# Sums of gates in six shared weight buffers, turns that meet, a norm by token tile and a re-ordered table in a transformer block

## The chip, the cores and the metric

The kernel runs on one core of one Trainium2 chip. The metric is the time of the device in microseconds (us) for one execution. Five engines run their own streams: TensorE (PE, matmuls), VectorE (DVE), ScalarE (ACT), GpSimd (POOL) and SyncE (SP, which issues most transfers). They meet at semaphores, and each works through its stream in the order in which it was written.

## What is computed

One block on x (256 tokens by 2048 channels), float32 throughout, with a conditioning vector c. Cut to what matters:

```python
mod = silu(c) @ w_ada + b_ada                  # w_ada 2048 x 12288
sh1, sc1, g1, sh2, sc2, g2 = split(mod, 6)     # parts 0..5 of the kernel
h = rms_norm(x, norm1_g) * (1 + sc1) + sh1
q, k, v, gb, gc, xt = split(h @ w_in, 6)       # each 256 x 1024; the kernel's q k v g c x
attn = softmax(mask(rms(q) @ rms(k).T / sqrt(128))) @ v     # 8 heads
conv = gb * causal_dwconv(gc * xt, conv_w, conv_b)          # 3 taps
mixed = concat(rms_norm(attn), rms_norm(conv))
x = x + g1 * (mixed @ w_out)                   # 2048 x 2048
h2 = rms_norm(x, norm2_g) * (1 + sc2) + sh2
u = causal_dwconv(h2 @ w_ffn_up, ffn_conv_w, ffn_conv_b)    # 2048 x 11264
x = x + g2 * ((silu(u_gate) * u_up) @ w_ffn_down)           # 5632 x 2048
```

## The kernel before

Nearly all of the work is one pass over 315 MB of weights. They arrive in raw tiles of 128x2048 float32 (1 MB, `raw`, a ring of 5 buffers, issued from SP's queue). A matmul on float32 is done as three faster ones: ACT rounds a tile to `hi` (L246), DVE takes the rest `lo` = raw - hi (L252), the activations are split in the same way (`h` and `hl`, `mixh` and `mixl`), and PE adds h x hi, hl x hi and h x lo. A ring of 3 holds hi and lo, and they are made two slots ahead of their use.

A **slot** is one weight tile, about 5.5 us of PE. There are 48 slots for `w_in` (0 to 47), 16 for `w_out` (48 to 63), 88 for `w_ffn_up` in pairs (64 to 151: a group of channels has two halves of k), and 48 for `w_ffn_down`. In slot i the loop at the end of the file first writes hi of slot i+2 and the small tasks that are due (before or after lo, by a class), then PE's matmuls of slot i, then the tiles of `w_ada` ("ada"). The table `CFG` holds the due slots, classes and orders, so the order on each engine follows from it.

What the change and the steps touch:

- **turns** (`CFG['turns']`): in which order the six products of `w_in` take their slots. Where the next turn of a product isn't in the next slot, its PSUM bank is emptied into an SBUF sum `pa_*` (ACT copy L424 the first time, DVE addition L426 after that).
- **ada**: the six vectors of the modulation. Some chunks are accumulated on PE (L297), the rest on DVE (L301 and L303, scalar times row plus sum, 16 rows of 128 of w_ada to a sum). The sums of the gates (parts 2 and 5) are 2048 wide and stand in a tile of their own; their bias comes by eight 1x512 transfers and eight additions (L325).
- **attention, conv**: mix tiles with their squares (L996, L1015); the last square's sum goes at once to PE (`ssA`, `ssC`, L1022), for the norms of the two halves. The conv's three taps are one ACT operation and two DVE ones (L1075 to L1078).
- **the end of w_out** (slots 62 and 63, bank `m('C', 3)`): DVE adds the product to x (L501, L506), ACT squares it (L508), the root, `n2d` and one matmul `n2b` (L606) spread 1/rms over the partitions, ACT copies it to `rB` (L610), and `h_chunks` write h2 (DVE L629, ACT L631, DVE L634), which the first `z` (L795) waits for. Four ada tiles (`fill`) are PE's work in between.
- **up**: each group's two slots hold their h x hi as 16 matmuls 512 wide (h and hl in one, L795) and h x lo as 16 that are 256 wide (L798); ACT and DVE add the two halves of a bank (`ub`, L685 and L688). With `direct` a slot's products go to one 256-wide half instead, and there is no addition on DVE.
- **spill**: the eight tiles of x are written to the output by ACT's queue (L541) between up slots, and read back for the end.

Of the kernel before, what the change touches and what calls it, by code (L numbers as in the profile page):

```python
# [1270 lines left out]
```

## Time and profile before

| | us |
|---|---|
| median of 3 runs (1179.96 to 1181.82) | 1180.21 |
| the profiled execution, its own time | 1182.36 |
| its span in the trace | 1180.5 |
| PE busy | 1153.6 |
| DVE busy | 934.8 |
| ACT busy | 620.3 |

The span is what the trace covers; the profiled execution took 1.86 us more than its span. Busy PE is not PE at its peak, since matmuls overlap; the spacing of equal matmuls in a row says what one costs. [...]

### The profile page before, as it was taken

The numbers are of one execution on the slowest core, as the hardware profiler recorded it, in microseconds if no ns is written. First come the engines' busy times: TensorE is split into PE (matmuls) and PEld (weight loads), VectorE is DVE, ScalarE is ACT, GpSimd is POOL, SyncE is SP. The second block draws the span as 40 slices with busy tenths as digits, with TensorE's granted clock in tenths as the row PEclk, the third lists the DMA queues.
The fourth block names the chain that finished last, engine by engine and source line by source line (L and its number), as shares of the span: only waits on it lengthen the run. The fifth ranks groups of instructions, "written<-read, shape, count | busy, mean of one in ns | idle before, by whom it ended". The sixth has DMA issues, their size and how long they took to land.

```text
span 1180.5 us, 15371 instructions
## 1 busy us (share of the span) xinstructions
PE 1153.6 (98%) x5971; PEld 964.6 (82%) x5971; DVE 934.8 (79%) x1060; ACT 620.3 (53%) x890; POOL 1.2 (0%) x8
## 2 busy tenths in 40 slices
PE   5999999999999999999999999999999999999998
PEld 3777788878877878888888888888888888888887
DVE  3588999999999989989988766887655676576876
ACT  5645265468584555476665434555444455335442
...
GB/s 364 382 348 389 384 344 376 414 366 319 319 280 308 285 297 330 384 237 155 178 222 259 372 324 319 234 195 179 194 230 172 189 179 208 234 210 203 135 169 89
DMA packets 189181, 317.98 MB, mean 269 GB/s; under 512 B 6922, under 2 KB 106028, under 8 KB 184756
## 3 DMA queue, kind: packets, MB, share of 16 engines
...
## 4 chain that ended last, share of the span: by engine, by line
PE 81%; DVE 10%; DMA 4%; ACT 2%; issue 1%; SPq 0%; ACTq 0%; DVEq 0%
PE z L795 23%; PE z L798 12%; DVE lo L252 4%; DVE ada L303 3%; DMA raw<-in_w_in_dram 2%; PE ada L297 1%; PE mg L414 1%; PE mg L415 1%; PE mg L412 1%; PE mx L414 1%; DMA raw<-in_w_ffn_up_dram 1%; PE mx L415 1%; PE mx L412 1%; DMA raw<-in_w_ada_dram 1%; PE mc L414 1%
## 5 line engine op out<-in xcount | busy, mean ns | idle before, releaser
L252 DVE TENSOR_TENSOR lo<-raw,hi 128x2048 fp32r<-128x2048 f32 (+2 forms) x204 | 448.2, 2204 | 141.5 <-ACT hi L246 125.4
L246 ACT ACTIVATE hi<-raw 128x2048 fp32r<-128x2048 f32 (+2 forms) x204 | 376.1, 1850 | 299.5 <-DMA raw<-in_w_in_dram 80.0
L795 PE MATMUL z<-h,hi 128*128 128x512 f32 x1408 | 329.7, 390 | 2.6 <-DVE h L634 2.0
L795 PEld LDWEIGHTS z<-h,hi 128*128 128x128 f32 x1408 | 261.1, 188 | 56.2 <-DVE h L634 1.4
L303 DVE SCALAR_TENSOR_TENSOR ada<-raw,csil,ada 128x512 f32<-128x512 f32 (+2 forms) x150 | 183.8, 1229 | 3.3 <-DMA raw<-in_w_ada_dram 0.2
L798 PEld LDWEIGHTS z<-h,lo 128*128 128x128 f32 x1408 | 174.8, 192 | 3.4
L798 PE MATMUL z<-h,lo 128*128 128x256 f32 x1408 | 176.0, 283 | 0.0
L688 DVE TENSOR_TENSOR ub<-z,ub 128x256 f32<-128x256 f32 x112 | 39.6, 417 | 34.4 <-ACT ub L685 34.3
L685 ACT ACTIVATE ub<-z 128x256 f32<-128x256 f32 x112 | 33.4, 383 | 35.3 <-PE z L795 35.3
L720 ACT ACTIVATE gh<-uy 128x512 fp32r<-128x512 f32 x22 | 13.9, 632 | 66.8 <-DVE uy L718 66.8
L702 ACT ACTIVATE uy<-ub,fc,fc 128x256 f32<-128x256 f32 x88 | 45.6, 600 | 1.9 <-DVE ub L693 1.9
L709 DVE SCALAR_TENSOR_TENSOR uy<-ub,fc,uy 128x254 f32<-128x254 f32 x88 | 42.5, 484 | 3.1
L707 DVE SCALAR_TENSOR_TENSOR uy<-ub,fc,uy 128x255 f32<-128x255 f32 x88 | 42.1, 479 | 0.1
L297 PE MATMUL ada<-raw,crep 128*32 128x256 f32 (+1 forms) x224 | 23.1, 530 | 7.6 <-DMA raw<-in_w_ada_dram 7.6
L714 ACT ACTIVATE uy<-uy 128x512 f32<-128x512 f32 x22 | 13.8, 627 | 29.7 <-DVE uy L709 29.7
L721 DVE TENSOR_TENSOR gl<-uy,gh 128x512 fp32r<-128x512 f32 x22 | 15.2, 693 | 15.4 <-ACT gh L720 15.4
L414 PE MATMUL mc<-hi,h 128*128 128x512 f32 x64 | 25.6, 400 | 1.1 <-ACT pa_x L424 1.1
L414 PE MATMUL mv<-hi,h 128*128 128x512 f32 x64 | 25.4, 397 | 0.7 <-ACT h L864 0.7
L414 PE MATMUL mg<-hi,h 128*128 128x512 f32 x64 | 25.7, 401 | 0.0
L414 PE MATMUL mx<-hi,h 128*128 128x512 f32 x64 | 25.4, 397 | 0.0
L414 PE MATMUL mk<-hi,h 128*128 128x512 f32 x64 | 25.3, 396 | 0.0
L415 PE MATMUL mq<-hi,hl 128*128 128x512 f32 x64 | 25.0, 391 | 0.2 <-DVE hl L869 0.2
...
## 6 DMA issues: line engine op xcount, KB each, us to landing
...
```

Of the source, the lines that this page charges most:

```text
L246: act(hi[:, :nk], t[:, :nk], AF.Copy)
L252: V.tensor_tensor(out=lo[:, :nk], in0=t[:, :nk], in1=hi[:, :nk].bitcast(F32), op=ALU.subtract)
L297: mm(self.acc[q:q + 32, :], crep[:, i, :], t[:, j, :], start=(r == 0 and j < 4), stop=(r == self.tiles - 1 and j >= self.rows - 4), tile_p ...
L303: V.scalar_tensor_tensor(out=self.acc, in0=t[:, j, :], scalar=csil[:, i:i + 1], in1=self.acc, op0=ALU.mult, op1=ALU.add)
L414: mm(o, a, hi[:, k, s], start=(first and k == 0), stop=False)
L415: mm(o, b, hi[:, k, s], start=False, stop=False)
L688: V.tensor_tensor(out=d, in0=zp[grp][ft][:, :256], in1=d, op=ALU.add)
L702: act(y, b, AF.Identity, bias=fcols[3][:, i:i + 1], scale=fcols[2][:, i:i + 1])
L707: V.scalar_tensor_tensor(out=y[:, 1:], in0=b[:, :255], scalar=fcols[1][:, i:i + 1], in1=y[:, 1:], op0=ALU.mult, op1=ALU.add)
L709: V.scalar_tensor_tensor(out=y[:, 2:], in0=b[:, :254], scalar=fcols[0][:, i:i + 1], in1=y[:, 2:], op0=ALU.mult, op1=ALU.add)
L795: mm(zp[grp][ft], hi[:, j, ft * P:(ft + 1) * P], h2T[k + j], start=begins and j == 0, stop=ends and j == 3)
L798: mm(zp[grp][ft][:, :256], lo[:, j, ft * P:(ft + 1) * P], h2T[k + j][:, :256], start=False, stop=False)
```

## The change

- The table has other numbers: turns, heads, due slots, classes, which raw tiles are loaded first (`x_first`) and where hi is written late (`hi_late`). The first loads, up to the eleventh raw tile, differ in one place only: slot 4's weights go ahead of an ada tile.
- `near` 1 to 3: a product's bank is kept if its next turn is up to three slots away. `direct` [0,0] to [1,0]: in groups 0 to 5 the slots of the first half of k write into 256-wide halves, so their 12 slots have 48 matmuls of 256 instead of 16 of 512 and 16 of 256.
- Buffers: raw 5 to 6, but the 2048-wide sums of the gates live in a raw tile (`home`, zeroed on POOL, with the bias row brought by POOL's queue), so five are left while a gate is summed. The eight bias transfers and additions go.
- One 256-wide chunk of part 1 is summed on DVE (16 operations 256 wide) instead of PE (two tiles of 16 matmuls).
- The sums of squares go to PE one slot later (`sslag`); squares and mix tiles of attention go in pairs, 512 wide.
- The last bank of w_out, and the last ones of w_ffn_down, are split in two halves of 256 with banks of their own; the norm after w_out goes by token tile, and `rB` is copied behind the first two chunks of h2.
- One tap of the short conv goes to ACT, the small vectors come by POOL's queue six slots earlier, and some small copies from PSUM move from DVE to ACT. The spills stand at slots 72, 74, 76, 78 instead of 69 to 72.

```diff
-         [4, 8, 512, False, 54, 7], [1, 2, 256, True, 0, 3], ...
+         ... [1, 8, 1024, False, 8, 12], [1, 2, 256, False, 1, 2], ...
- 'bufs': [42, 6, 5, 3, 3],
+ 'bufs': [38, 6, 6, 3, 5],
+ 'taps': [1, 0, 0],
+ 'sslag': 1,
- 'near': 1,
+ 'near': 3,
- 'direct': [0, 0],
- 'spill': [5, 1],
+ 'direct': [1, 0],
+ 'spill': [8, 2],
...
     def load_next():
         if pending:
+            if isinstance(pending[0], Ada):
+                pending.pop(0).home()
+                return
...
+        def home(self):
+            what = f"ada{self.part}_{self.c0}"
+            self.acc = sb.tile([P, 4, 512], F32, tag="raw", bufs=N_RAW, name=what).rearrange("p a b -> p (a b)")
+            nc.gpsimd.memset(self.acc, 0.0)
+            a = self.part * D + self.c0 * P
+            nc.gpsimd.dma_start(self.acc[0:1, :], b_ada[0:1, a:a + self.n])
...
+        one(0, slice(0, 512), 0)
+        one(1, slice(0, 256), 1)
+        root(0, 0)
+        one(1, slice(256, 512), 2)
+        nrm["p"] = bank("n2b")
+        diag(0)
+        root(1, 2)
+        diag(1)
...
-        p = bank("n2b")
-        mm(p[:, :256], ones, d, start=True, stop=True)
+        for t in range(2):
+            mm(p[:, t * P:(t + 1) * P], ones, nrm["d", t], start=True, stop=True)
...
+        ks = list(range(cut[0]))
+        h2_chunks(ks[:2], p[:, :256])
         act(rB[0], p[:, :256], AF.Copy)
-        h2_chunks(range(cut[0]), p[:, :256])
+        h2_chunks(ks[2:], rB[0])
...
+            if CFG["sslag"]:
+                at(now[0] + CFG["sslag"], ss_cols, w)
```

ACT at slots 1 to 3, before (`hi` is the rounding of a weight tile, `pa_x` and `pa_c` empty the banks of slots 2 and 3, `adae` a bank of an ada sum):

```order
L313 ACTIVATE adae_2_400<-ada_2_312 128x256
L246 ACTIVATE hi<-raw 128x2048
L424 ACTIVATE pa_x_456<-mx_402 128x512
L424 ACTIVATE pa_x_458<-mx_403 128x512
L424 ACTIVATE pa_x_460<-mx_416 128x512
L424 ACTIVATE pa_x_462<-mx_417 128x512
L313 ACTIVATE adae_2_468<-ada_2_323 128x256
L424 ACTIVATE pa_c_510<-mc_470 128x512
L424 ACTIVATE pa_c_512<-mc_471 128x512
```

and now (the banks of slots 1 and 2 are `mc` and `mv`):

```order
L255 ACTIVATE hi<-raw 128x2048 x2
L431 ACTIVATE pa_c_380<-mc_333 128x512
L431 ACTIVATE pa_c_382<-mc_334 128x512
L431 ACTIVATE pa_c_384<-mc_347 128x512
L431 ACTIVATE pa_c_386<-mc_348 128x512
L431 ACTIVATE pa_v_440<-mv_392 128x512
L431 ACTIVATE pa_v_442<-mv_393 128x512
L431 ACTIVATE pa_v_444<-mv_406 128x512
L431 ACTIVATE pa_v_446<-mv_407 128x512
L329 ACTIVATE adae_2_448<-ada_2_314 128x256
L255 ACTIVATE hi<-raw 128x2048
```

The banks of slot 2 were emptied behind hi of slot 5; they are now emptied ahead of it, behind hi of slot 4.

PE at the end of slot 49, before (`m('A', 1)` and `m('A', 0)` are banks of w_out, `adab` spreads a gate, `trg` transposes for the conv):

```order
L412 MATMUL m('A', 1)1_2937<-lo,mix_2150 128x512
L369 MATMUL adab_0_2964<-ada_0_1535,ones 128x512
L1022 MATMUL ssA<-ones,sq 128x1 x2
L1064 MATMUL trg_2982<-ident,pa_g_392 128x128
L1064 MATMUL trg_2982<-ident,pa_g_394 128x128
```

and now, at the end of slot 51:

```order
L422 MATMUL m('A', 1)1_2867<-hi,mixl 128x512
L419 MATMUL m('A', 1)0_2866<-lo,mixh 128x512
L419 MATMUL m('A', 1)1_2867<-lo,mixh 128x512
L419 MATMUL m('A', 1)0_2866<-lo,mixh 128x512
L419 MATMUL m('A', 1)1_2867<-lo,mixh 128x512
L419 MATMUL m('A', 1)0_2866<-lo,mixh 128x512
L419 MATMUL m('A', 1)1_2867<-lo,mixh 128x512
L419 MATMUL m('A', 1)0_2866<-lo,mixh 128x512
L419 MATMUL m('A', 1)1_2867<-lo,mixh 128x512
L1052 MATMUL ssA<-ones,sq 128x1 x4
```

The matmul of the summed squares stands a slot behind the one in which DVE writes them.

ACT at slots 70 to 74, before (`ub` empties a bank of up, `ada ... adaz` is a sum of the modulation, `h2f` and `h_12` make h2's chunks 12 and 13, the DMAs are spills):

```order
L541 DMA out_dram<-x_03_2573 128x512
L541 DMA out_dram<-x_13_2581 128x512
L685 ACTIVATE ub_4176<-z_0_4081 128x256
L685 ACTIVATE ub_4176<-z_1_4082 128x256
L685 ACTIVATE ub_4177<-z_2_4083 128x256
L685 ACTIVATE ub_4177<-z_3_4084 128x256
L348 ACTIVATE ada_12_3949,adaz<-adac_12_4235 128x128 x4
L246 ACTIVATE hi<-raw 128x2048
L348 ACTIVATE ada_8_3789,adaz<-adac_8_4286 128x128 x4
L647 ACTIVATE h2f<-h2f,B_93,A_92 128x256 x2
L649 ACTIVATE h_12_4298<-h2f 128x2x256
```

and now:

```order
L355 ACTIVATE ada_8_3940,adaz<-adac_8_4430 128x128 x4
L528 DMA out_dram<-x_01_2915 128x512
L528 DMA out_dram<-x_11_2923 128x512
L669 ACTIVATE h2f<-h2f,B_93,A_92 128x256 x2
L671 ACTIVATE h_12_4445<-h2f 128x2x256
L669 ACTIVATE h2f<-h2f,B_93,A_92 128x256 x2
L671 ACTIVATE h_14_4451<-h2f 128x2x256
L255 ACTIVATE hi<-raw 128x2048 x2
L653 ACTIVATE h_8_4520<-h2f,B_93 128x256
```

Two spills stand directly ahead of the work on h2's chunks 8 to 15, where before the last spill was some twelve instructions ahead of it.

## Rows read from the trace of the kernel before

**Rows 1.** Page: each engine's busy us, share of the span, instructions.

```profile
PE 1153.6 (98%) x5971; PEld 964.6 (82%) x5971; DVE 934.8 (79%) x1060; ACT 620.3 (53%) x890; POOL 1.2 (0%) x8
```

**Rows 2.** Busy by stretch: length, PE, PEld, DVE, ACT, POOL, PEclk, DMA share, GB/s.

```profile
0.00:28.00 28.00, 13.68 (x102) 8.02 (x102) 8.68 (x24) 13.68 (x20) 1.22 (x8) 1.00 0.97 364
28.00:60.00 32.00, 30.81 (x179) 22.59 (x180) 18.52 (x20) 20.57 (x29) 0.00 (x0) 1.00 1.01 382
60.00:250.00 190.00, 188.96 (x873) 148.60 (x872) 177.14 (x172) 95.42 (x172) 0.00 (x0) 1.00 0.98 377
250.00:440.00 190.00, 186.90 (x923) 151.27 (x921) 177.34 (x226) 121.59 (x236) 0.00 (x0) 1.00 0.84 304
440.00:520.00 80.00, 77.38 (x447) 67.48 (x448) 72.80 (x103) 45.72 (x75) 0.00 (x0) 1.00 0.92 326
520.00:1176.00 656.00, 655.90 (x3452) 566.69 (x3450) 478.77 (x516) 323.34 (x361) 0.00 (x0) 1.00 0.62 213
```

**Rows 3.** What PE waited for: us in total, times, longest.

```profile
PE z L795 <- DVE h L634: 2.0, 2, 1.2
...
PE ssA L1022 <- DVE sq L1015: 1.1, 1, 1.1
PE mc L414 <- ACT pa_x L424: 1.1, 1, 1.1
...
PE ssC L1022 <- DVE cv L1015: 0.7, 1, 0.7
PE n2b L606 <- DVE n2d L604: 0.6, 1, 0.6
PE z L795 <- ACT ada L348: 0.5, 1, 0.5
```

**Rows 4.** Chain that ended last: start, length, what, here matmuls in a row.

```profile
515.66 3.83 PE z L798 x32
519.49 7.28 PE z L795 x32
```

**Rows 5.** Timeline of PE: start, length, operation [idle before, releaser], ada tiles.

```profile
34.04 1.93 PE L297 MATMUL ada<-raw,crep 128*32 128x256 f32 x32
35.90 0.50 PE L414 MATMUL mg<-hi,h 128*128 128x512 f32 x1
```

**Rows 6.** Timeline of ACT around slot 3.

```profile
51.58 1.91 ACT L246 ACTIVATE hi<-raw 128x2048 fp32r<-128x2048 f32 x1 [5.09 <-DMA raw<-in_w_in_dram]
53.40 2.04 ACT L424 ACTIVATE pa_x<-mx 128x512 f32<-128x512 f32 x4
```

**Rows 7.** Timelines of PE and DVE where up begins.

```profile
434.20 3.64 PE L297 MATMUL ada<-raw,crep 128*32 128x512 f32 x32
...
439.55 0.87 DVE L629 SCALAR_TENSOR_TENSOR h2f<-x1T,A,n2b 128x256 f32<-128x256 f32 x2 [1.27 <-ACT rB L610]
...
441.14 3.92 PE L795 MATMUL z<-h,hi 128*128 128x512 f32 x16 [1.18 <-DVE h L634]
```

**Rows 8.** DVE by shape: busy us, mean ns, idle before.

```profile
L688 DVE TENSOR_TENSOR ub<-z,ub 128x256 f32<-128x256 f32 x112 | 39.6, 417 | 34.4 <-ACT ub L685 34.3
...
L629 DVE SCALAR_TENSOR_TENSOR h2f<-x1T,A,rB 128x256 f32<-128x256 f32 x4 | 1.8, 479 | 0.0
```

**Rows 9.** The bias additions of the gates: what DVE waited for, us, times.

```profile
  DMA gb<-in_b_ada_dram: 1.1, 2
```

**Rows 10.** Timelines of DVE and PE around slot 66, whose lo is the first row's second.

```profile
449.16 4.49 DVE L252 TENSOR_TENSOR lo<-raw,hi 128x2048 fp32r<-128x2048 f32 x2
...
452.75 4.30 PE L795 MATMUL z<-h,hi 128*128 128x512 f32 x16
456.89 3.27 PE L798 MATMUL z<-h,lo 128*128 128x256 f32 x26
```

**Rows 11.** Timelines of ACT and PE around the spills and slot 76.

```profile
489.37 1.92 ACT L246 ACTIVATE hi<-raw 128x2048 fp32r<-128x2048 f32 x1 [5.18 <-DMA out_dram<-x]
...
511.75 0.47 PE L795 MATMUL z<-h,hi 128*128 128x512 f32 x1 [0.79 <-DVE h L634]
```

More of the change, by code (lines that the diff above doesn't have):

```diff
@@ L572, in go @@
         def go(hi, lo, part=part, f=f, k=k, tf=n == len(seq) - 1):
-            mm_tok((part, f), hi, lo, [mixT[k + j] for j in range(4)], 4, k % 8 == 0, k % 8 == 4, tf, tf and CFG["tail1"])
+            mm_tok((part, f), hi, lo, [mixT[k + j] for j in range(4)], 4, k % 8 == 0, k % 8 == 4, tf, (part, f) == ("C", 3))
             if k % 8 == 4:
@@ L659, in tile_block, with conv3 @@
     at(N_OUT, evac_c, 3)
+    at(N_OUT, norm2)
     at(N_OUT + CFG["tr3"], tr_out, 3)
-    at(N_OUT, norm2)
+    if any(e[2] == 2048 and e[0] == G1 for e in CFG["ada"]):
+        at(N_OUT + 2, load_next)
     for f in range(4):
         at(N_OUT + CFG["spill"][0] + f * CFG["spill"][1], spill, f)
+    def conv3(b, y, w, bias, i, taps):
+        for j in range(2):
+            s = slice(j * 256, j * 256 + 256)
+            act(y[:, s], b[:, s], AF.Identity, bias=bias[:, i + j:i + j + 1], scale=w[2][:, i + j:i + j + 1])
+        for d in (1, 2):
+            if d > taps:
+                for j in range(2):
+                    o, v = (e[:, j * 256:j * 256 + 256] for e in (y, b))
+                    V.scalar_tensor_tensor(out=o[:, d:], in0=v[:, :256 - d], scalar=w[2 - d][:, i + j:i + j + 1],
+                                           in1=o[:, d:], op0=ALU.mult, op1=ALU.add)
+            else:
+                z = t2k("tap")
+                for j in range(2):
+                    s = slice(j * 256, j * 256 + 256)
+                    act(z[:, s], b[:, s], AF.Copy, scale=w[2 - d][:, i + j:i + j + 1])
+                V.tensor_tensor(out=pair(y)[:, :, d:], in0=pair(z)[:, :, :256 - d], in1=pair(y)[:, :, d:], op=ALU.add)
     ub, uy = {}, {}
@@ L1005, in att_o, with ss_cols @@
         mm(p[:, 128:256], v[1], pt[:, 256:], start=False, stop=True)
-        att[h] = (p, mix_tile(h, p[:, :256], gain["A"][:, h:h + 1]))
-    sums = {}
+        both = h // 2 in two
+        if not both:
+            two[h // 2] = t2k("my"), t2k("sq")
+        y, q = two[h // 2]
+        one = slice(h % 2 * 256, h % 2 * 256 + 256)
+        act(y[:, one], p[:, :256], AF.Copy, scale=gain["A"][:, h:h + 1])
+        act(q[:, one], p[:, :256], AF.Square)
+        if both:
+            hi, lo = t2k("mixh", F32R), t2k("mixl", F32R)
+            act(hi, y, AF.Copy)
+            V.tensor_tensor(out=lo, in0=y, in1=hi.bitcast(F32), op=ALU.subtract)
+            for j, s in enumerate((slice(0, 256), slice(256, 512))):
+                mixT[h // 2 * 2 + j] = hi[:, s], lo[:, s]
+    sums, two = {}, {}
+    def ss_cols(w):
+        p = bank("ss" + w)
+        n = sums[w].shape[1] // 256
+        for t in range(2):
+            for j in range(n):
+                a = j * 256 + t * P
+                mm(p[:, t:t + 1], sums[w][:, a:a + P], ones[:, 0:1], start=j == 0, stop=j == n - 1)
+        V.tensor_copy(ssA if w == "A" else ssC, p[:, :2])
+        done.add("ss" + w)
     def add_square(w, q, first, last):
@@ L1016, in add_square @@
         if last:
-            p = bank("ss" + w)
-            n = sums[w].shape[1] // 256
-            for t in range(2):
-                for j in range(n):
-                    a = j * 256 + t * P
-                    mm(p[:, t:t + 1], sums[w][:, a:a + P], ones[:, 0:1], start=j == 0, stop=j == n - 1)
-            V.tensor_copy(ssA if w == "A" else ssC, p[:, :2])
+            if CFG["sslag"]:
+                at(now[0] + CFG["sslag"], ss_cols, w)
+            else:
+                ss_cols(w)
     def att_q(h):
-        _, q = att.pop(h)
-        done.add(f"ss{h}")
-        add_square("A", q, len([1 for g in range(8) if f"ss{g}" in done]) == 1,
+        assert h % 2 and h in mixT and h - 1 in mixT
+        done.update((f"ss{h - 1}", f"ss{h}"))
+        add_square("A", two[h // 2][1], len([1 for g in range(8) if f"ss{g}" in done]) == 2,
                    all(f"ss{g}" in done for g in range(8)))
     def out_norm(w, s):
-        assert all(f"ss{h}" in done for h in range(8)) if w == "A" else {"cq0", "cq1"} <= done
+        assert "ss" + w in done
         r = const.tile([P, 2], F32, name="r" + w)
```

266 lines of the change are left out of this document (120 added, 146 removed), and 25 rows, old and new, of the table CFG.

## The prediction

> **What bounds the kernel now.** I read the page first: PE is busy for 1153.6 of 1180.5 us, DVE for 934.8, ACT for 620.3 [rows 1]. So the question for every edit is what it does to PE's stream. Next the table of stretches, which shows where PE has room at all [rows 2]. Idle PE is 28.00 - 13.68 = 14.3 us in the first 28 us, 1.2 us to 60, 1.0 to 250, 3.1 to 440, 2.6 to 520, 0.1 from 520 to 1176, and 4.5 us in the tail. The first stretch waits for the first loads, which the change leaves nearly as they are, and the tail is the last addition and its store. What the change can win lies between 28 and 520 us: 1.2 + 1.0 + 3.1 + 2.6 = 7.9 us of idle time, and it can go no further than that by removing waits. DVE is close to full there (177.14 of 190 us in two stretches), but PE doesn't wait for a weight's hi or lo anywhere: no row of PE's waits names them, and what the list has are single waits of 0.5 to 1.2 us [rows 3]. The third view is therefore that list, and the fourth the timelines around each wait. One profiled execution gives all rows; its own time was 1182.36 us and the median 1180.21, so I apply the sum of the differences to the median. A difference under 0.2% (2.4 us) is about what a measurement of this kernel can't tell from none.
>
> **What PE gets to do more or less.** A matmul 256 wide costs 3.83 / 32 = 0.120 us in a row of its kind, one 512 wide 7.28 / 32 = 0.2275 us [rows 4]. *Direct*: 12 slots with 48 x 0.120 = 5.75 us instead of 16 x 0.2275 + 16 x 0.120 = 5.55 us, so 12 x 0.19 = +2.3 us. This lies on the path, as PE never rests there. *Halves*: a 512-wide matmul in two costs 2 x 0.1197 - 0.2275 = 0.012 us more; there are 24 more such splits at the end of w_out and 18 at the end of w_ffn_down, +0.5 us. *Two more small matmuls* for the sums of squares, +0.2 us as an estimate from the 0.120 us row. *The ada chunk that leaves PE*: 32 matmuls from 34.04 until the next slot's first at 35.90 are two tiles, so 0.93 us a tile [rows 5] and -1.9 us for two. PE works there almost without a gap (30.81 of 32 us from 28 to 60 us) [rows 2], so it counts in full. Sum on PE: 2.3 + 0.5 + 0.2 - 1.9 = **+1.1 us**.
>
> **The waits that go.** *mc, 1.1 us* [rows 3]: in slot 3 PE wants a bank that ACT empties behind hi of slot 5, and that hi waits 5.09 us for its weights, until 51.58; the copies start at 53.40 [rows 6]. Now the bank is emptied ahead of that hi. What is late next is the chain that makes h2's predecessor, chunks 2 and 3 of h, for slot 5; it hangs on the same hi and on DVE's lo behind it, and I find it within some 0.5 us of PE. So -1.0 us, with -0.6 as the poor end. *ssA and ssC, 1.1 + 0.7 = 1.8 us* [rows 3]: both matmuls wait for a sum that DVE finishes at that moment. One slot (5.5 us) later the sum is long there; the norm behind it is due a slot later too, and the first bank that needs it is not emptied before. -1.8 us. *The norm after w_out, 0.6 + 1.18 us* [rows 3, 7]: n2b waits for n2d, and after it DVE waits 1.27 us for ACT's copy rB. The copy now stands behind the first two chunks of h2, which read the bank. The token tile that is ready first has its root early, so n2d is done about when the four ada tiles are. What stays is h2's own chain: DVE, ACT, DVE. I take -1.0 us; between -0.5 and -1.6. *z's bank, 0.5 us* [rows 3]: the bank comes from an ada sum that ACT reads late; the change has those sums elsewhere. -0.5 us. *z at slot 76, 0.79 us* [rows 11]: the same chain of h2 chunks; DVE's lo before it comes as before, but 4 additions of 0.417 us [rows 8] are gone from just ahead of it. Half of it, -0.4 us. Sum: 1.0 + 1.8 + 1.0 + 0.5 + 0.4 = **-4.7 us**, from -3.4 to -5.7.
>
> **What DVE and ACT get.** DVE loses 24 additions at 0.417 us [rows 8], 10.0 us, ten bank additions, and the eight bias additions; it gains 16 operations for the ada chunk. A 256-wide operation of that kind is 0.479 us [rows 8], so 7.7 us. They come between 28 and 60 us, where DVE is busy 18.52 of 32 us [rows 2]: covered. If the cover were gone, slot 5's chunks of h would be late by part of it. ACT gets eight short operations for the tap, seven copies and three table loads, and is busy 620.3 of 1180.5 us [rows 1]: covered. What DVE saves behind 60 us is worth nothing directly, since PE doesn't wait for lo there; it buys room for a PE that is ahead by some 3 us from slot 5 on. The weights must come that much sooner as well: the load is at 377 GB/s from 60 to 250 us [rows 2], and the new order asks for less ahead of most slots (one to three tiles fewer), for one tile more at slots 25 to 28. The sixth raw buffer doesn't raise the rate. I put 0 to 2.5 us on such lost ground.
>
> **New waits.** In a direct slot the first products with lo come after two matmuls and not after sixteen, 3.6 us sooner. The closest is slot 66: its lo ends near 451.4 (the first of the pair, 449.16 + 2.24), PE begins the slot at 452.75 and takes lo at 456.89 [rows 10]. Now it wants it near 453 less PE's lead. But the ada chunk that DVE had ahead of that lo is moved off, and h2 is done a little earlier, so I expect no wait; up to 1 us. Together with the lost ground, and spills and table loads: **+0.8 us**, from 0 to +3.5.
>
> **The sum**: +1.1 - 4.7 + 0.8 = -2.8 us, so about 1182.4 - 2.8 = 1179.6 us for a run like the profiled one and 1180.2 - 2.8 = **1177.4 us** for the median. With the ends: 1.1 - 5.7 + 0 = -4.6 and 1.1 - 3.4 + 3.5 = +1.2, 1175.6 to 1181.4.
>
> **Rivals.** *More comes off than the named waits.* Of the 7.9 us of idle time I count 4.7; the rest are pieces of under 0.5 us where PE turns from one kind of work to another behind ACT or DVE. If the new order hides most of them (-7.0 in all, and none come new), it ends at 1180.2 + 1.1 - 7.0 = 1174.3 us. For it: DVE gets lighter from slot 30 on. Against: the changes at those places are only orders, and an ordered wait is usually replaced by a small one. *The gain is eaten.* PE's lead after slot 5 runs into the loads at slots 20 to 35, where DMA is already at a share of 0.98 [rows 2], and everything won before is given back: what is left is +1.1 (direct and halves count in full, the ada tiles not: +3.0) - 1.8 - 1.0 - 0.5 = -0.3, so 1179.9 us. For it: the share. Against it: no wait of PE for hi, lo or raw between 28 and 520 us in the list. *Slower, by a stall of ACT's queue.* ACT waited 5.18 us behind a spill at 489.37 [rows 11], with nothing due just then. The spills now stand directly ahead of h2's chunks 8 to 15, which slot 76 needs at 511.75, and there PE is already waiting 0.79 us for that chain [rows 11]. A stall of the same 5.18 us there costs all of it: 1180.2 - 2.8 + 5.2 = 1182.6 us, which is slower by 0.2%. It decides from 2.8 us on, where the gain is gone, and is slower by 0.2% from 5.2 us. For it: same queue, same kind of transfer, and ACT hands on in order. Against it: the spills now come two slots apart instead of one, so the queue has twice the time to be free again. *The row of a gate's sum is late.* It now comes by GpSimd's queue, into a raw tile, and DVE's first sum waits for it, with lo queued behind. The trace of before has no transfer of that queue; the nearest row is the old bias transfer, for which DVE waited 1.1 us in two waits [rows 9]. One latency of that kind for each of two gates, all on PE, would be 1180.2 - 2.8 + 1.1 = 1178.5 us; at the bound of below nothing it is hidden, as the tile is asked for several slots ahead. [...]
>
> **How the numbers follow.** The forecast, 1177.4 us: 0.52. It has about 0.33 under the line at 1177.85 and 0.19 over. More comes off, 1174.3: 0.16, faster. Eaten, 1179.9: 0.15, same but for 0.02. ACT's stall, 1182.6: 0.13, of which 0.11 slower. The late row, 1178.5: 0.04, same but for 0.03, slower where a whole chain hangs on the row. So faster 0.33 + 0.16 = 0.49, same 0.19 + 0.13 + 0.02 + 0.01 = 0.35, slower 0.02 + 0.11 + 0.03 = 0.16. The range takes in the first rival down to 1173.5 and the sum's poor end and most of the stall up to 1182.6; about a tenth is left out on each side. The forecast's own range is 1175.6 to 1181.4.
>
> **What would show it.** In the trace of the changed kernel: no wait of PE for ssA, ssC or an empty bank at slot 3; the first z some 6 us behind the start of the four ada tiles (it was 441.14 - 434.20 = 6.9) [rows 7]; direct slots of 5.75 us; two ada tiles fewer on PE before 60 us. PE's idle time from 28 to 520 us should be near 7.9 - 4.7 + 0.8 = 4 us. I would be wrong if that idle time stays at 8 us (a lead that the loads or DVE take back), if PE waits by name for hi or lo (direct slots, slots 20 to 35), or if ACT waits behind `out_dram` near slot 76.

## The result, and the profile after

The changed kernel takes 1172.99 us (median of 4 runs, 1171.32 to 1173.29), beside 1180.09 us for the kernel before on the same chip (4 runs, 1179.02 to 1181.82). The ratio is 0.9936, with a 95% interval from 0.9918 to 0.9953. That is 7.1 us less where 2.8 were forecast, and just below the lower end of the range, 1173.5. The profiled execution took 1173.29 us with a span of 1171.5.

The page of the changed kernel, each engine's busy time, and the shares of the chain that ended last:

```profile
PE 1151.7 (98%) x6179; PEld 977.4 (83%) x6179; DVE 914.9 (78%) x1022; ACT 629.7 (54%) x910; POOL 12.0 (1%) x23
...
PE 97%; DMA 1%; DVE 1%; ACT 0%; SPq 0%; issue 0%; ACTq 0%
```

PE's busy time fell by only 1.9 us against [rows 1]. What went is the time between its matmuls. The table of stretches (length, PE, PEld, DVE, ACT, POOL, PEclk, DMA share, GB/s):

```profile
28.00:60.00 32.00, 31.88 (x165) 23.75 (x166) 24.83 (x35) 23.64 (x35) 0.00 (x0) 1.00 1.05 406
60.00:250.00 190.00, 189.76 (x877) 150.61 (x878) 174.88 (x161) 99.87 (x183) 4.91 (x6) 1.00 0.99 377
250.00:440.00 190.00, 189.62 (x996) 157.60 (x995) 177.22 (x229) 127.57 (x249) 0.00 (x0) 1.00 0.88 317
440.00:520.00 80.00, 80.00 (x627) 78.06 (x626) 66.96 (x74) 46.31 (x74) 0.00 (x0) 1.00 0.94 327
```

Idle PE is 0.12 + 0.24 + 0.38 + 0 = 0.7 us from 28 to 520 us; it was 7.9 [rows 2], and the prediction said that about 4 would stay. The list of what PE waited for (us in total, times, longest) has only the start left, and two pieces of 0.2 us:

```profile
PE ada L313 <- DMA raw<-in_w_ada_dram: 8.1, 2, 7.4
PE pv_ccol L193 <- DMA vcb<-in_c_dram: 4.2, 1, 4.2
PE adac L348 <- ACT adae L329: 1.5, 2, 1.0
PE mg L421 <- ACT h L897: 0.7, 1, 0.7
PE z L814 <- ACT h L653: 0.2, 1, 0.2
PE adac L348 <- ACT hi L255: 0.2, 1, 0.2
```

**Where the 9 us lie.** In both traces I took the distance from the start of one matmul to the start of the next and subtracted the pitch of its kind (0.2275 us for 512 columns, 0.120 for 256 [rows 4]). What remains is time above pitch. It sees more than the idle time does: the end of a matmul is modelled, 0.39 us behind its start where the next one starts after 0.2275, so every gap hides some 0.16 us. How the small matmuls between the products are counted is a choice: with other pitches for them the 10.5 us below come out between 9.4 and 10.9, and the 4.9 between 4.5 and 4.9. Summed by slots, with the time of the pitches themselves ("work") behind; the kernels e1 to e18 are the experiments below:

| us above pitch in slots | 0-20 | 20-35 | 35-52 | 52-64 | 64-76 | rest | sum | work |
|---|---|---|---|---|---|---|---|---|
| before | 5.2 | 0.0 | 5.2 | 3.2 | 2.7 | 0.1 | 16.3 | 1128.5 |
| after | 3.0 | 0.6 | 0.3 | 1.1 | 0.7 | 0.1 | 5.8 | 1129.8 |
| e1 | 5.8 | 0.0 | 5.3 | 2.2 | 2.2 | 0.2 | 15.7 | 1129.3 |
| e2 | 4.0 | 6.0 | 5.4 | 7.7 | 0.7 | 0.1 | 23.8 | 1129.8 |
| e3 | 3.0 | 0.7 | 0.3 | 1.7 | 4.3 | 0.1 | 10.1 | 1127.5 |
| e4 | 3.1 | 0.7 | 7.2 | 8.9 | 0.7 | 0.1 | 20.7 | 1129.8 |
| e5 | 3.0 | 0.6 | 1.0 | 1.1 | 0.7 | 0.0 | 6.5 | 1129.8 |
| e6 | 3.0 | 1.7 | 0.3 | 1.1 | 0.7 | 0.1 | 7.0 | 1129.8 |
| e7 | 3.4 | 0.6 | 0.3 | 1.5 | 0.7 | 0.1 | 6.6 | 1129.8 |
| e8 | 3.0 | 0.6 | 0.4 | 1.1 | 0.9 | 0.1 | 6.1 | 1129.0 |
| e9 | 3.0 | 0.6 | 0.4 | 1.1 | 0.7 | 0.0 | 5.8 | 1129.8 |
| e10 | 3.4 | 0.6 | 0.7 | 2.2 | 0.7 | 0.1 | 7.7 | 1129.8 |
| e11 | 4.5 | 2.3 | 7.7 | 3.7 | 0.7 | 0.1 | 19.0 | 1129.8 |
| e12 | 3.2 | 0.6 | 0.3 | 1.1 | 0.7 | 0.0 | 6.0 | 1131.7 |
| e13 | 3.9 | 3.0 | 8.4 | 4.1 | 0.7 | 0.1 | 20.2 | 1129.8 |
| e14 | 3.9 | 1.8 | 9.4 | 3.6 | 0.7 | 0.0 | 19.4 | 1129.8 |
| e15 | 4.1 | 4.3 | 7.6 | 4.2 | 2.2 | 1.8 | 24.2 | 1131.6 |
| e16 | 4.7 | 1.3 | 13.0 | 9.0 | 2.3 | 1.0 | 31.2 | 1128.5 |
| e17 | 3.0 | 0.7 | 5.9 | 1.1 | 0.7 | 0.1 | 11.5 | 1129.8 |
| e18 | 4.7 | 0.0 | 4.0 | 3.1 | 1.9 | 0.1 | 13.8 | 1128.5 |

From slot 0 to the last matmul the trace has 1147.5 us before and 1138.3 after: 1.3 us more work and 10.5 us less above pitch. The forecast had +1.1 and -3.9. The largest part by far, 4.9 us, is in slots 35 to 52, for which the forecast had credited only the wait for ssA. The experiments look for what did that. The trace's 9.2 us and the medians' 7.1 may differ because slot 0 begins anywhere between 25.5 and 28.1 us in the twenty traces, of whatever kernel; both traces compared here began late (28.09 and 28.12), and the median runs may not have. I therefore judge parts of the change by the time from slot 0 on, of one trace each.

### The profile page after: what moved, and what is told of

Same layout as the page of the kernel before. It is cut to its first block, busy times and chain, and to the rows that moved or that the text cites. A ratio compares the mean times of both kernels' runs of the same rounds, so it can differ in the third digit from the quotient of the medians.

```text
span 1171.5 us, 15784 instructions
## 1 busy us (share of the span) xinstructions
PE 1151.7 (98%) x6179; PEld 977.4 (83%) x6179; DVE 914.9 (78%) x1022; ACT 629.7 (54%) x910; POOL 12.0 (1%) x23
## 4 chain that ended last, share of the span: by engine, by line
PE 97%; DMA 1%; DVE 1%; ACT 0%; SPq 0%; issue 0%; ACTq 0%
PE z L828 24%; PE z L831 12%; PE z L814 6%; PE ada L313 2%; PE mc L421 1%; PE mg L421 1%; PE mx L421 1%; PE mk L421 1%; PE mg L422 1%; PE mv L421 1%; PE mq L421 1%; PE mc L422 1%; PE mx L422 1%; PE mq L422 1%; PE mv L422 1%; PE mk L422 1%
## 5 line engine op out<-in xcount | busy, mean ns | idle before, releaser
L828 PE MATMUL z<-h,hi 128*128 128x512 f32 x1216 | 283.8, 390 | 0.0
L828 PEld LDWEIGHTS z<-h,hi 128*128 128x128 f32 x1216 | 225.8, 188 | 45.3
L319 DVE SCALAR_TENSOR_TENSOR ada<-raw,csil,ada 128x512 f32<-128x512 f32 (+3 forms) x167 | 195.3, 1175 | 3.5
L831 PEld LDWEIGHTS z<-h,lo 128*128 128x128 f32 x1216 | 151.0, 192 | 3.0
L831 PE MATMUL z<-h,lo 128*128 128x256 f32 x1216 | 152.0, 283 | 0.0
L699 DVE SCALAR_TENSOR_TENSOR uy<-ub,fc,uy 128x254 f32<-128x254 f32 (+1 forms) x176 | 71.3, 477 | 0.2
L814 PE MATMUL z<-h,hi 128*128 128x256 f32 x384 | 69.9, 284 | 0.4 <-ACT h L653 0.2
L731 DVE TENSOR_TENSOR ub<-z,ub 128x256 f32<-128x256 f32 x88 | 31.2, 417 | 41.6 <-ACT ub L728 41.6
L814 PEld LDWEIGHTS z<-h,hi 128*128 128x128 f32 x384 | 59.9, 192 | 0.8 <-ACT h L653 0.5
L814 PE MATMUL z<-h,lo 128*128 128x256 f32 x192 | 54.3, 283 | 0.0
L728 ACT ACTIVATE ub<-z 128x256 f32<-128x256 f32 x88 | 26.3, 384 | 27.6 <-PE z L828 27.6
L814 PEld LDWEIGHTS z<-h,lo 128*128 128x128 f32 x192 | 36.8, 192 | 0.0
L421 PE MATMUL mg<-hi,h 128*128 128x512 f32 x64 | 25.5, 399 | 0.7 <-ACT h L897 0.7
L421 PE MATMUL mq<-hi,h 128*128 128x512 f32 x64 | 25.3, 395 | 0.0
```

The source lines that it names most:

```text
L319: V.scalar_tensor_tensor(out=self.acc, in0=t[:, j, :], scalar=csil[:, i:i + 1], in1=self.acc, op0=ALU.mult, op1=ALU.add)
L421: mm(o, a, hi[:, k, s], start=(first and k == 0), stop=False)
L699: V.scalar_tensor_tensor(out=o[:, d:], in0=v[:, :256 - d], scalar=w[2 - d][:, i + j:i + j + 1], in1=o[:, d:], op0=ALU.mult, op1=ALU.add)
L731: V.tensor_tensor(out=d, in0=zp[grp][ft][:, :256], in1=d, op=ALU.add)
L814: mm(o, w[:, j, a], h2T[k + j][:, v * 256:v * 256 + 256], start=begins and j == 0 and w is hi and not v, stop=ends and j == 3 and w is lo)
L828: mm(zp[grp][ft], hi[:, j, ft * P:(ft + 1) * P], h2T[k + j], start=begins and j == 0, stop=ends and j == 3)
```

## Code, table, buffers

Theory A: the gain is in the orders that the table sets. Theory B: it is in the buffers and the code, above all the sixth raw tile.

**e1, the changed code with the old table.** Turns, ada, due slots, classes and lists as before, raw buffers 6, and the new options off:

```diff
- 'bufs': [38, 6, 6, 3, 5],
...
+ 'bufs': [42, 6, 6, 3, 3],
...
- 'taps': [1, 0, 0],
- 'sslag': 1,
...
+ 'taps': [0, 0, 0],
+ 'sslag': 0,
...
- 'near': 3,
+ 'near': 1,
...
- 'direct': [1, 0],
...
+ 'direct': [0, 0],
...
```

> The changed code with the table of before (near 1, no direct slots, sums of squares at once, no tap on ACT; six raw buffers, gates' sums in raw tiles). Theory A (order): PE's time above its pitch from slot 0 to the last matmul was 16.3 us before and 5.9 us after, and most of the 10.5 us is won by where the table puts tasks, so with the old table only the norm by token tile (about 1 us) and the bias additions remain: 1178 to 1179.5 us, PE's time above pitch 14 to 15.5 us. Theory B (buffers and load): the sixth raw buffer and the lighter DVE and SP queues bring it: 1175 to 1176.5 us, time above pitch under 11 us.

Measured: 1178.55 us, ratio 0.9987 [0.9978, 0.9997]. By time that is some 1.5 us less than before, but from slot 0 on it is 1147.7 us beside 1147.5, so with the old table the code and the sixth buffer together bring next to nothing, and slots 35 to 52 lose what they lost. One of PE's waits there:

```profile
PE as L989 <- ACT kT L982: 2.6, 1, 2.6
```

**e2, the changed kernel with five raw buffers.**

```diff
- 'bufs': [38, 6, 6, 3, 5],
+ 'bufs': [38, 6, 5, 3, 5],
```

> The changed kernel with five raw buffers, four while a gate is summed. Theory A: PE does not wait for a weight's hi or lo, so 1173 to 1174 us and no wait of PE for hi, lo or raw over 0.5 us. Theory B: weights come late where a gate is summed (slots 25 to 50), 1176 us or more, with waits of ACT's hi for raw that reach PE.

Measured: 1187.75 us, 1.0056 [1.0039, 1.0074], slower than before. So the new orders need the sixth buffer, though with the old ones (e1) it and the code bring nothing: neither theory is right alone. PE's waits now include (with 2.6 us for a raw tile of ada in slots 20 to 28):

```profile
PE ssC L1052 <- DVE cv L1061: 3.3, 1, 3.3
PE ap L1016 <- ACT s L1008: 2.9, 1, 2.9
```

## Single edits with a price in the forecast

**e3, no direct slots.**

```diff
- 'direct': [1, 0],
+ 'direct': [0, 0],
```

> The changed kernel with no direct slots: 12 slots of 5.55 instead of 5.75 us on PE, and 24 more additions (10 us) on DVE at slots 64 to 77. If DVE has room there: 2.3 us faster than the change, 1170.7 us, with z starts at slot 76 some 2.3 us earlier. If the direct slots are what keeps DVE out of PE's way: the wait for h2 at slot 76 comes back (0.8 to 3 us), 1172.5 to 1174 us.

Measured: 1173.81 us, 0.9945 [0.9929, 0.9961]. PE's work fell by 2.3 us, exactly the price that the forecast put on the 12 slots, but time above pitch rose by 4.3 us, mostly in slots 64 to 76. PE's waits here, the first of them one of before:

```profile
PE z L828 <- DVE h L656: 2.0, 2, 1.1
...
PE adac L348 <- DVE ub L731: 0.9, 1, 0.9
```

The direct slots are not a pure cost: they spare DVE the additions and give it time to make h2, worth 2.0 us net in the traces (1140.3 us from slot 0 on, beside 1138.3).

**e4, sums of squares in the slot in which they are due, as before.**

```diff
- 'sslag': 1,
+ 'sslag': 0,
```

> The changed kernel with the sums of squares sent to PE in the slot in which DVE writes them. Theory of the forecast: the two waits of 1.1 and 0.7 us for ssA and ssC come back, and nothing else: 1.8 us slower than the change, 1174.8 us. Rival: the new order of tasks writes the squares early enough that PE meets them ready: within 0.5 us of the change.

Measured: 1184.89 us, 1.0041 [1.0026, 1.0056]. The two waits are 3.4 and 4.3 us here, more than the 1.1 and 0.7 of before [rows 3], and the loss, 14.9 us from slot 0 to the end, is nearly twice their sum. The timeline of PE behind the first of them, and the table of stretches (PEclk is the third number from the end of a row), show the other half:

```profile
347.04 1.69 PE L1052 MATMUL ssA<-ones,sq 128*128 128x1 f32 x8 [3.39 <-DVE sq L1061]
348.59 0.77 PE L421 MATMUL m('A', 1)0_2866<-hi,mixh 128*128 128x512 f32 x1
349.16 0.63 PE L422 MATMUL m('A', 1)0_2866<-hi,mixl 128*128 128x512 f32 x1
349.59 0.63 PE L421 MATMUL m('A', 1)1_2867<-hi,mixh 128*128 128x512 f32 x1
```

```profile
343.00:347.00 4.00, 0.65 (x3) 0.19 (x2) 3.90 (x3) 3.64 (x5) 0.00 (x0) 1.00 0.86 284
347.00:350.00 3.00, 2.96 (x11) 2.72 (x12) 1.23 (x3) 0.00 (x0) 0.00 (x0) 0.53 1.05 406
350.00:353.00 3.00, 3.00 (x8) 2.31 (x7) 2.96 (x4) 0.00 (x0) 0.00 (x0) 0.50 1.04 421
```

Behind the wait the granted clock is 0.50 for some microseconds, and the matmuls stand 0.43 us apart instead of 0.2275.

**e5, e6, e7, e8: four small ones.** e5 puts back the heads' due numbers and classes, e6 the rule that a bank is kept only for the next slot's turn, e7 the copy of `rB` ahead of h2's first chunks, and e8 takes the direct slots off groups 1 and 2.

```diff
- 'heads': [2, 7, 8, 4, 5, 5, 4, 4],
- 'head_steps': [1, 1, 2, 3, 5],
+ 'heads': [4, 4, 7, 2, 4, 5, 5, 4],
+ 'head_steps': [1, 1, 2, 3, 4],
...
- 'near': 3,
+ 'near': 1,
...
-        ks = list(range(cut[0]))
-        h2_chunks(ks[:2], p[:, :256])
         act(rB[0], p[:, :256], AF.Copy)
-        h2_chunks(ks[2:], rB[0])
+        h2_chunks(range(cut[0]), p[:, :256])
...
+                if seg == 0 ... and grp in (0, 3, 4, 5):
```

> The changed kernel with the attention steps of before: the due slots of the eight heads, the distances of their steps and the classes of three steps. PE's time above its pitch from slot 35 to 51 was 5.2 us before and 0.3 us in the change, and DVE is equally busy in both (177 of 190 us from 250 to 440 us). Theory A (order): where the heads' steps stand decides it, so waits for ACT (as, ap) or for the last squares (ssA) come back, 3 us or more above pitch there, 1176 us or more. Theory C (work): the lighter vector work of attention (pairs, taps, kept banks) decides it: under 1 us above pitch there, 1173 to 1174 us.

> The changed kernel with banks kept only for the next slot (near 1): ten more additions of 0.68 us, 6.8 us, on DVE before slot 48. Theory A (order, with DVE's slack of some 4 us kept): no wait of PE over 0.5 us, within 1 us of the change, 1173 to 1174 us. Theory C (work): DVE falls behind and PE waits for lo or for what is queued behind it, 1175 us or more.

> The changed kernel with ACT's copy rB ahead of h2's first two chunks, as before the change; the rest of the norm by token tile stays. The forecast's reading of the 1.27 us that DVE waited for rB: the first z starts 0.5 to 0.7 us later. Rival: h2's first chunks wait for DVE's own chain anyway, under 0.2 us. Either way 1173 to 1174 us; the start of z in the trace decides.

> The changed kernel with direct slots in groups 0, 3, 4 and 5 alone. Without any direct slot PE did 2.3 us less work from slot 64 to 76 and stood 3.6 us more above its pitch, at the start of group 0 and around groups 3 to 5. If the direct slots pay only where h2 or a bank is late, groups 1 and 2 can do without: 4 slots, 0.8 us less work and no wait more, 0.8 us less from slot 64 to slot 76. If it is the ten microseconds of DVE additions that matter wherever they stand, a wait of 0.5 us or more comes at slots 72 to 76.

Measured: 1172.27, 1172.25, 1171.23 and 1171.71 us, none told apart from the changed kernel's 1172.99, since slot 0 alone begins up to 2.6 us apart. From the traces: e5 costs 0.7 us, in slots 35 to 52 as looked for but far from the 4.9; e6 costs 1.1 in slots 20 to 28; e7 costs 0.4 where up begins, its first z waiting 0.66 us for ACT's h instead of 0.24; e8 has 0.8 us less work and loses 0.2, so from slot 0 on it is the shortest of all, 1137.8 us. That half a microsecond isn't told apart by time.

**e12, the chunk of part 1 back on PE.**

```diff
- ... [1, 2, 256, False, 1, 2],
+ ... [1, 2, 256, True, 1, 2],
```

> The changed kernel with the 256-wide chunk of part 1 summed on PE again: two ada tiles, 32 matmuls, more on PE, and 16 operations 256 wide less on DVE. As the forecast has it: 2 x 0.93 = +1.9 us of work before slot 6 and nothing else, 1174.9 us. Rival (these tiles fill a time in which PE would stand anyway, as it waits for the first loads): from 0 to +0.5 us, 1173.0 to 1173.5. Rival (DVE's 16 operations were not free, and a chunk of h comes sooner without them): -0.5 to 0, 1172.5 to 1173.0.

Measured: 1173.22 us, 0.994 [0.9924, 0.9957]. From slot 0 to the last matmul it is 1140.3 us, 2.0 more than after, with 1.9 more work: the forecast's price. In the run's time it can't be seen, since slot 0 began at 25.57 us in this trace and at 28.12 in the other.

## What empties slots 35 to 52

There the attention of the heads begins. The chain of a head is: `as` on PE (scores), the maximum `m` on DVE, `s` on ACT (exponential), the reciprocal on DVE, `s` on ACT again, and `ap` on PE a slot after `as`.

**e9, the old due numbers of the roots of q and k; e10, these and those of heads and conv.**

```diff
- 'qk': [[3, 5], [3, 7]],
+ 'qk': [[4, 5], [0, 7]],
...
-         'qk_stat': 0,
+         'qk_stat': 1,
...
-         'qk_root': 0,
+         'qk_root': 2,
...
- 'conv': [[1, 3, 3, 2, 7, 9, 8, 9], [1, 2, 3, 2, 1, 3, 5, 5]],
+ 'conv': [[1, 2, 2, 3, 6, 7, 8, 8], [1, 2, 2, 2, 1, 2, 4, 6]],
```

> The changed kernel with the old due numbers and classes of the roots and statistics of q and k alone (their squares, roots and scaled copies come a slot or two later on ACT and DVE). In slots 35 to 52 the kernel before lost 5.17 us above the pitch of its matmuls, the changed one 0.33, and neither the code nor the heads' steps account for it. Theory Q (q and k are ready a slot earlier, so no head waits for kT or for s): PE waits for kT or s come back by name, slots 35 to 52 rise by 2 to 3 us, and the time goes from 1173.0 to 1175 or 1176. Theory L (the order of the loads and where hi is written late): nothing moves, 1172.5 to 1173.5, and less than 0.5 us above the pitch in slots 35 to 52. Theory T (the turns of the products themselves, which give PE a slot that needs nothing new): as L, and the next two runs don't move either.

> The changed kernel with the old due numbers and classes of q and k, of the heads and of the conv, while turns, loads, buffers and code stay as changed. Theory Q with the heads (which alone brought 0.7 us): slots 35 to 52 at 3 to 4.5 us above pitch, 52 to 60 unchanged, 1176 to 1178. Theory C (the conv's steps decide, since the last of its squares was due at that moment before): more than the run before it by over 1 us, most of it in slots 43 to 60. Theory T (turns) or L (loads): slots 35 to 52 under 1.5 us, 1173 to 1174.

Measured: 1171.92 us, 0.9925 [0.9911, 0.994], and 1172.56 us, 0.9933 [0.9918, 0.9948]. Theory Q falls: 0.4 us above pitch in slots 35 to 52, and 0.7 with heads and conv. When the small tasks are due decides little there; in slots 52 to 64 heads and conv cost e10 1.1 us.

**e11, both lists of before (`x_first`, `hi_late`); e13, `hi_late` alone; e14, `x_first` alone.** `x_first` lists the slots whose ada tiles are loaded ahead of the weight tile; the expectation of e14 says it the other way round. In these slots hi and lo of the slot after next also stand behind the ada sums on ACT and DVE, and `hi_late` doesn't act there. In the slots of `hi_late` hi stands behind the small tasks. So neither list is an order of loads alone.

```diff
- 'x_first': [1, 3, 4, 5, 9, 10, 12, 13, 15, 16, 18, 19, 21, 23, 24, 26, 28, 31, 39, 43, ...
+ 'x_first': [4, 5, 7, 9, 11, 12, 15, 16, 18, 19, 20, 22, 23, 24, 27, 31, 32, 37, 39, 42, ...
- 'hi_late': [5, 8, 10, 12, 14, 15, 16, 17, 18, 19, 20, 21, 24, 27, 28, 35, 39, 40, 45, ...
+ 'hi_late': [0, 5, 6, 11, 13, 15, 16, 19, 21, 22, 25, 32, 37, 39, 43, 44, 45, 48, 49, ...
```

> The changed kernel with the old order of loads behind the first ones and the old list of slots in which hi is written late. Theory L: slots 35 to 52 rise by 2 us or more above pitch, with PE waiting by name for hi, lo or for a small task behind a late hi; 1175 to 1178. Theories Q and T: under 0.7 us there; then the time is 1172.5 to 1173.8, or something is lost at other slots, where a task stands behind a hi that is now early.

> The changed kernel with the old list of slots in which hi is written late, that is behind the small tasks of its slot. Theory H (a small task that PE needs stands behind hi in ACT's order in the wrong slots; the copies of kT and s are the ones that PE waited for by name): slots 35 to 52 rise from 0.3 to 4 us or more above pitch, and most of the loss of the run with both lists is here, 1178 to 1184 us. Rival O (the order of weight and ada tiles decides, so that raw tiles come late): under 1 us of change, 1172.5 to 1174.

> The changed kernel with the old list of slots in which a weight tile goes ahead of the ada tile. Theory O: PE waits for what hangs on a raw tile, 1177 to 1184 us, most of it in slots 3 to 52. Theory H: 1172.5 to 1174.5, and slots 35 to 52 under 1 us above pitch. Neither alone (the two lists fit one another): both runs below 1176, and the loss of the two together, 13 us, isn't their sum.

Measured: 1184.6 us, 1.0033 [1.0022, 1.0045]; 1185.86 us, 1.005 [1.0032, 1.0068]; 1184.69 us, 1.0038 [1.0024, 1.0051]. Each list alone costs as much as both together. Theories H and O, which wanted one of the two, both miss, and so does "neither alone". In all three `ap` waits 3.5 to 4.4 us for `s`, and the timelines of the engines show whose lateness it is. The head's chain in e14 (`m` is DVE's), with the operation that DVE did just ahead of `m`:

```profile
240.92 0.38 PE L990 MATMUL as<-kT,qT 128*128 128x128 f32 x2
...
246.03 2.34 DVE L319 SCALAR_TENSOR_TENSOR ada<-raw,csil,ada 128x2048 f32<-128x2048 f32 x1
248.29 0.28 DVE L996 TENSOR_REDUCE m<-as 128x1 f32<-128x128 f32 x1
...
252.25 1.09 PE L1016 MATMUL ap<-ident,s 128*128 128x128 f32 x3 [4.37 <-ACT s L1008]
```

and the same chain in the changed kernel:

```profile
241.26 0.38 PE L990 MATMUL as<-kT,qT 128*128 128x128 f32 x2
...
240.91 2.35 DVE L319 SCALAR_TENSOR_TENSOR ada<-raw,csil,ada 128x2048 f32<-128x2048 f32 x1
243.17 0.29 DVE L996 TENSOR_REDUCE m<-as 128x1 f32<-128x128 f32 x1
...
247.00 0.50 ACT L1009 ACTIVATE s<-s,r 128x256 f32<-128x256 f32 x1
...
248.06 0.49 PE L1016 MATMUL ap<-ident,s 128*128 128x128 f32 x3
```

`m` comes 1.9 us behind `as` in the changed kernel, 7.4 in e14, and 6.6 in e11 and e13. DVE works through its queue of lo and ada sums, and `m` stands in it; whoever makes DVE late makes `ap` late. The kernel before lay between:

```profile
245.69 0.49 PE L957 MATMUL as<-kT,qT 128*128 128x128 f32 x2 [0.82 <-ACT kT L950]
...
249.54 0.28 DVE L963 TENSOR_REDUCE m<-as 128x1 f32<-128x128 f32 x1
...
253.51 0.84 PE L983 MATMUL ap<-ident,s 128*128 128x128 f32 x3 [0.32 <-ACT s L975]
```

Its wait for kT leads back to DVE too. ACT writes kT behind the squares of k and one hi, and the squares waited for an addition that stands in DVE's queue behind an ada sum:

```profile
239.80 0.31 ACT L915 ACTIVATE sqj<-pa_k 128x128 f32<-128x128 f32 x1 [1.03 <-DVE pa_k L426]
```

Gap by gap, the 4.9 us that slots 35 to 52 lost in the kernel before and not in the changed one are 2.0 ahead of `ap`, 1.6 ahead of ssA, 1.1 ahead of `as` (where the wait for kT is) and small pieces.

What DVE lost on the way is in its own list of waits. From 28 to 245 us, before, after (the two longest rows), and e14:

```profile
DVE lo L252 <- ACT hi L246: 20.7, 13, 4.1
```

```profile
DVE lo L261 <- ACT hi L255: 7.4, 7, 2.4
DVE hl L902 <- ACT h L900: 7.2, 6, 3.2
```

```profile
DVE lo L261 <- ACT hi L255: 16.7, 12, 3.7
```

The wait of lo for hi is 14.6 us in e11, 18.7 in e13, 11.6 in e2 and 17.3 in e1. Its fall of 13.3 us is not all won, since other waits rose, that of hl for ACT's h first. DVE's whole busy time from 28 to 245 us, before and after (length, DVE, PEclk, DMA share, GB/s):

```profile
28.00:245.00 217.00, 190.66 (x188) 1.00 0.99 377
28.00:245.00 217.00, 196.01 (x192) 1.00 0.99 381
```

So DVE stands idle 5.3 us less in the changed kernel, and with an old list (e11, e13, e14) it is busy for 188.2 to 190.4 us, no more than before. `m` is 6.4 us sooner than before (249.54 to 243.17): some 5.4 us by less idle time, and 1.0 by less work ahead of it. PE comes to `as` 4.4 us sooner, which leaves 1.9 us against `as`.

**e15, turns, ada sums and both lists of before as one set in the changed kernel; e16, the kernel before with the two new lists.**

```diff
-CFG = {'ada': [[0, 12, 512, False, 17, 4], ...
+CFG = {'ada': [[4, 0, 1024, False, 25, 15], ...
...
- 'turns': [['g', 0, 2], ['c', 0, 2], ...
+ 'turns': [['v', 0, 2], ['g', 0, 2], ...
...
```

> The changed kernel with turns, ada sums and both lists of before as one set; buffers, classes, due numbers and code stay as changed. Theory F (lists, turns and ada sums only have to fit one another, and the gain at slots 35 to 52 comes from the due numbers and classes of the small tasks): slots 35 to 52 at 0.3 to 1.5 us above pitch, 1173 to 1176 us. Theory S (the set itself is what was gained): 4 to 6 us above pitch there, as before, and the bank's wait at slot 3 comes back too; 1177 to 1181 us.

> The kernel before with the two new lists and nothing else. If the lists are better by themselves, slots 35 to 52 fall from 5.2 to under 2.5 us and the time goes to 1176 to 1178. If they fit only their own turns (theories F and S): as before or slower, 1180 to 1192 us.

Measured: 1190.52 us, 1.0082 [1.0064, 1.01], and 1196.6 us, 1.0139 [1.0119, 1.0158]. Both are slower than either kernel, and e15 slower than theory S allowed. The lists are no improvement by themselves; they fit one table and spoil another. In e16 PE waits for the ends of DVE's chains:

```profile
PE ssA L1022 <- DVE sq L1015: 5.1, 1, 5.1
...
PE ssC L1022 <- DVE cv L1015: 3.9, 1, 3.9
```

**e17, the changed kernel with 4.6 us more on DVE; e18, the kernel before with 6.0 us less.** All orders stay. e17 adds zero times the gate's sum to that sum, twice; in the trace the two operations are at 197.60 and 205.90 us, earlier than expected, and take 2.29 us each. e18 leaves out most of three rows of weights of the gate's sum, so it no longer computes the block: three operations take 0.35 us instead of 2.35.

```diff
                     V.scalar_tensor_tensor(out=self.acc, in0=t[:, j, :], scalar=csil[:, i:i + 1],
                                            in1=self.acc, op0=ALU.mult, op1=ALU.add)
+                    if self.part == 2 and r in (1, 2):
+                        V.scalar_tensor_tensor(out=self.acc, in0=self.acc, scalar=0.0,
+                                               in1=self.acc, op0=ALU.mult, op1=ALU.add)
...
+                    m = 128 if self.part == 2 and r in (1, 2, 3) else self.n
-                    V.scalar_tensor_tensor(out=self.acc, ...
+                    V.scalar_tensor_tensor(out=self.acc[:, :m], ...
```

> The changed kernel with two more operations on DVE, 2048 wide and 2.35 us each, behind the ones at 211.54 and 224.26 us (each adds zero times the gate's sum to itself). Theory D (DVE, nearly full from 100 us on, is what PE waits for, by way of the head's reductions; its idle time behind hi is what the order of loads costs): DVE has some 0.8 us of idle time between there and the first head's reductions, so these come 3.5 to 4 us later, PE waits for s at ap for 3 to 3.5 us where it waited none, and slots 35 to 52 go from 0.3 to 5 to 9 us above pitch as in the runs with an old list; 1178 to 1184 us. Rival N (DVE has room, since PE never waits for lo by name): the operations are hidden, slots 35 to 52 under 1.5 us, 1173 to 1174.

> The kernel before with three operations on DVE cut from 2048 to 128 wide, those at 211.95, 223.15 and 236.83 us (the gate's sum leaves out most of three rows of weights). Theory D: the roots, reductions and sums that ap and as wait for come up to 4 us sooner; the 2.5 us that PE loses at as and ap go, the waits for ssA and ssC a hundred us later stay, so slots 35 to 52 fall from 5.2 to 2 to 3.5 us and the time by 2 to 3 us, to 1177 to 1178. Rival N: nothing beyond 0.5 us, 1179.5 to 1180.5. Between the two: DVE only stands longer behind hi, and a part of it arrives.

Measured for e17: 1178.61 us, 0.9977 [0.9967, 0.9987], 5.6 us more than the changed kernel, and 5.6 us from slot 0 on too, all of it in slots 35 to 52. The head's chain:

```profile
241.06 0.38 PE L993 MATMUL as<-kT,qT 128*128 128x128 f32 x2
...
245.30 2.35 DVE L319 SCALAR_TENSOR_TENSOR ada<-raw,csil,ada 128x2048 f32<-128x2048 f32 x1
247.57 0.29 DVE L999 TENSOR_REDUCE m<-as 128x1 f32<-128x128 f32 x1
...
251.54 1.09 PE L1019 MATMUL ap<-ident,s 128*128 128x128 f32 x3 [3.52 <-ACT s L1011]
```

`m` is 6.5 us behind `as` instead of 1.9, so all of the 4.6 us arrived, and PE, which waits for no lo anywhere, stood 3.5 us. The other 2 us are the clock, as in e4 (the same columns, here with PE alone):

```profile
251.50:254.50 3.00, 2.89 (x8) 0.56 1.05 351
```

Measured for e18: 1179.38 us, 0.9997 [0.9987, 1.0006], no difference by time. In its trace it is 1145.0 us from slot 0 on, 2.5 less than before: 1.2 of it in slots 35 to 52, which fall from 5.2 to 4.0, 0.5 in 0 to 20 and 0.8 in 64 to 76. The waits for kT and s are gone from the list, but DVE stands 24.8 us behind hi instead of 20.7, so 4.1 of the 6.0 us were lost there, and `m` is only 1.8 us sooner against slot 0. Theory D's 2 to 3.5 us in slots 35 to 52 was too hopeful, and "between the two" holds. So e17 shows that DVE's time decides in the changed kernel; in the kernel before it moved the same waits, but only a part of it reached them.

## Why the prediction was too small, by its steps

- **PE's work, +1.1 us: right.** The pitches sum to +1.3; e3 has the direct slots at 2.3, e12 the ada tiles at 1.9. In the trace the direct slots are 576 = 12 x 48 matmuls; the fourth runs from 449.72 to 455.48 us, 5.76, and the first three are longer by the small work between them.
- **The waits that go, -4.7 us: the mechanisms were right, the sum was too small.** It left out one wait as long as those that it took: 0.8 us of `as` for kT stands in PE's list of before, and "the rest are pieces of under 0.5 us" is wrong. Every wait named has gone, but for 0.2 us of the first z's. Time above pitch in slots 0 to 20 fell by 2.2 us (the forecast had 1.0 for mc). Where up begins, z starts 431.50 - 426.09 = 5.4 us behind the four ada tiles, and was 6.9 [rows 7], so 1.5 where -1.0 was taken and -1.6 was the bound; the four rows of PE:

```profile
426.09 3.64 PE L313 MATMUL ada<-raw,crep 128*32 128x512 f32 x32
429.67 0.72 PE L626 MATMUL n2b<-n2d,ones 128*128 128x128 f32 x4
430.23 1.04 PE L542 MATMUL x1t<-ident,x 128*128 128x128 f32 x8
431.50 0.91 PE L814 MATMUL z<-h,hi 128*128 128x256 f32 x2 [0.24 <-ACT h L653]
```

  In slots 64 to 76 it fell by 2.0 us, where 0.9 were taken for the two waits: the half of 0.79 us taken for z at slot 76 was too cautious, as e3 shows what the direct slots do for that chain; even the whole would have given 1.3.
- **The step that failed** is the term put at nothing by "What DVE saves behind 60 us is worth nothing directly, since PE doesn't wait for lo there". It gave slots 35 to 52 no more than ssA's 1.1 us. PE doesn't wait for lo, but for `m`, `r`, the additions ahead of kT and the squares, which stand in the same queue behind lo. With the new turns, lists and sixth buffer DVE reached `m` 6.4 us sooner, 1.9 of them against `as`, and 4.9 us of time above pitch went: 1.6 at ssA, and 3.1 at `ap` and `as`, for which the forecast had nothing. Most of the 6.4 us is not work saved but idle time saved, which the forecast didn't look at. e17 shows the link by itself. Which orders spare DVE that time was not settled. With either old list (e13, e14) or without the sixth buffer (e2) the gain is lost; both new lists in the old table (e16), or the code with the buffer (e1), don't bring it; the due numbers (e5, e9, e10) matter little. Turns and ada sums were not tried by themselves.
- **"It can go no further than that by removing waits", 7.9 us: false.** Idle time fell by 7.2 us, but time above pitch by 10.5, since a gap of 0.5 us shows as some 0.3 us idle behind a modelled end. The wait for kT and pieces under 0.5 us, which I left uncounted, hold much of the rest.
- **New waits and lost ground, +0.8 us: nearly none came.** Slots 20 to 35 have 0.6 us above pitch, where before had none. For the lead that the loads would take back, the share of DMA is 0.99 from 60 to 250 us and PE still waits for nothing. ACT has no wait behind a spill between 430 and 520 us. DVE has none for the gates' bias rows, whose two transfers land 4.5 and 2.5 us after their issue, so the late row, which would have shown as such a wait, did not come either.
- **The rivals.** "More comes off", with -7.0 us and 1174.3, came nearest, and had 0.16: idle time fell by 7.2. Its reason, pieces of under 0.5 us, covers only a part; the rest is the head's chain, which no rival named, so that its number fits is in part luck. Against it I had put that "an ordered wait is usually replaced by a small one". Here little replaced them, the 0.6 us in slots 20 to 35.
